# One decoder block on one core: state-space pieces placed at four sums of each mixer pair, norm and operand arithmetic moved from GpSimd to VectorE

## The chip, the cores and the metric

The kernel runs on one core of a Trainium2 chip. The metric is device microseconds from the start to the end of one execution, as a median over runs. The profile is one execution; its times are microseconds (us) from the start of its span. PE is TensorE, DVE is VectorE, ACT is ScalarE, POOL is GpSimd, and SP is the engine that here only issues DMAs.

## The reference

The block works on 1024 tokens of 1024 features, all in float32:

```
x = LN1(ALPHA*x + 0.5*swiglu(x, ffn1_w_in, ffn1_w_out))
mix = token_mixer(x)                    # proj = x @ mix_w_in, 4096 columns in six parts:
    z      = causal_conv3(cc * ch)      #   short convolution branch
    y_conv = (cb * z) @ conv_w_out
    s      = gelu(s5_scan(su))          #   diagonal state-space branch, 32 groups of 64 states
    y_ssm  = ga * sigmoid(gb)           #   ga, gb = split(s @ w_glu)
    out    = (sigmoid(g_conv)*y_conv + sigmoid(g_ssm)*y_ssm) @ mix_w_out
x = LN2(ALPHA*x + mix)
x = LN3(ALPHA*x + 0.5*swiglu(x, ffn2_w_in, ffn2_w_out))
x = LN4(ALPHA*x + (p @ ple_w_in) * sigmoid(x @ ple_w_gate))
```

## The kernel before

**Arithmetic.** Every float32 product is made of three passes of PE: each operand is split into a rounded high part (ACT, L175) and the remainder as a low part (DVE, L176, `Wl` for weights, `x..l` for activations), and PE adds high by high, high by low and low by high. A weight block `Ws` is loaded by SP, becomes `Wh` on ACT and then `Wl` on DVE, with three buffers of each, and only then can PE finish the product that uses it.

**Pairs.** The two feed-forward inputs and the mixer's input projection are computed by a Winograd scheme (class `Pair`) of seven products of 12 matmuls each for two column blocks. POOL forms the sums of weights (`s`, L79, L84, L88, L96), DVE adds the products up in four sums (L87, L92, L99, L101). The activations need seven operands `x11`, `xt1`, `xt2`, `xt3`, `x21`, `x22`, `xt4`; four of them are differences of blocks. For the first feed-forward they come from DMA and are formed in `first_operands.later` (L422 to L438) at some 17 to 50 us: one half of them (j = 0) on DVE, one half (j = 1) on POOL. For the mixer and for the second feed-forward they are formed in `winograd_sink` while the norm ahead of them ends (two sinks, some 695 to 750 us and 1280 to 1335 us): here j = 0 is POOL's, j = 1 DVE's.

**Mixer.** 16 pairs: two for the state-space input, four gates, six for the convolution, four gates. Into these pairs the state-space branch is fed in pieces: `ssm_quarter` is a generator with 12 steps for each of four quarters, and after each pair from the second on the loop takes three steps (four from the eleventh on). After the last pair the region "ssm" is closed and "res2" opened in its place, into which the eight blocks `gc` are loaded (`acc<-gc`, L1061, 512 KB each). Then come the products with `conv_w_out`, whose weights are `in_w_co`, and the state-space result `s` is loaded and split to `sT`.

**Last loop.** For each of eight rows of 128 tokens (in two cuts of 512 columns, in three for the last) PE forms the gate `pg` (24 matmuls, L1243) and the embedding `pe` (6 matmuls, L1248, two PSUM buffers `pt`), ACT the sigmoid `sg` (L1251), DVE the product (L1252) and the sum into `acc2` (L1253), and then the row's norm. Ahead of that, `affine(...)`'s `apply` multiplies the row by the third norm's gain and adds its bias (L315, L316), the left half on DVE, the right half on POOL.

**Order.** The code is written in order, and a scheduler of the tile framework then places the instructions of all engines by its own estimate of when each is ready. `tc.issue_after(ins)` keeps what is written inside it behind `ins` on that instruction's engine; without it the scheduler may hoist work ahead of other rows'. DMAs are all issued by SP, in one order, and SP waits at each for what that DMA needs.

Of the kernel before, what the change touches and what calls it, by code (L numbers as in the profile page):

```python
# [12 lines left out]
ALU = mybir.AluOpType  # L13
# [8 lines left out]
EARLY = 5  # L22
FIRST = [f for i in range(NPAIR) for f in (i, NPAIR + i)]
MAGIC = 12582912.0
TICKS = 3
HALVES = (slice(0, 512), slice(512, 1024))


# [77 lines left out]
class Block:  # L106
# [194 lines left out]
    def affine(self, g, b, tag):  # L301

        if tag == "A8":
            both = self.t("A8", [P, 2, D], name="gb")
            gb = [both[:, v, 512 * h:512 * h + 512] for v in range(2) for h in range(2)]
        else:
            gb = [self.t(tag, [P, 512], name="gb") for _ in range(4)]
        for i, part in enumerate(gb):
            self.nc.sync.dma_start(part, (g, b)[i // 2][i % 2 * 512:i % 2 * 512 + 512].partition_broadcast(P))

        def apply(t):
            for h in range(2):
                sl = slice(h * 512, (h + 1) * 512)
                eng = (self.nc.vector, self.nc.gpsimd)[h]
                eng.tensor_tensor(t[:, sl], t[:, sl], gb[h], ALU.mult)  # L315
                eng.tensor_tensor(t[:, sl], t[:, sl], gb[2 + h], ALU.add)  # L316
        return apply


# [20 lines left out]
    def winograd_sink(self, xs, gb):  # L340

        kept = []
        gps = self.nc.gpsimd

        def put(name, y, i, j, eng=None):
            cols, ks = slice((i % 2) * 256, (i % 2 + 1) * 256), slice(2 * j, 2 * j + 2)
            hi, lo = xs[name]
            self.split(y, hi[:, ks, cols], lo[:, ks, cols], eng)

        def sink(i, pair):  # L350
            if i < 2:
                kept.append([self.t("H", [P, 4, 256], name="y") for _ in range(2)])
                for kh in range(2):
                    for j in range(2):
                        y = kept[i][kh][:, 2 * j:2 * j + 2]
                        self.features(pair, gb, 4 * kh + 2 * j, y)
                        put(("11", "21")[kh], y, i, j, None if (kh, j) == (0, 1) else gps)
                return
            for j in range(2):
                b11, b21 = (kept[i - 2][kh][:, 2 * j:2 * j + 2] for kh in range(2))  # L360
                b12, b22 = self.t("T", [P, 2, 256], name="b12"), self.t("T", [P, 2, 256], name="b22")
                t1 = self.t("T", [P, 2, 256], name="t1")
                self.features(pair, gb, 2 * j, b12)
                eng = (gps, self.nc.vector)[j]
                eng.tensor_tensor(t1, b12, b11, ALU.subtract)
                put("t1", t1, i, j)
                self.features(pair, gb, 4 + 2 * j, b22)
                put("22", b22, i, j)
                eng.tensor_tensor(b12, b22, b12, ALU.subtract)
                put("t3", b12, i, j)  # L370
                eng.tensor_tensor(t1, b22, t1, ALU.subtract)
                put("t2", t1, i, j)
                eng.tensor_tensor(t1, b21, t1, ALU.subtract)
                put("t4", t1, i, j)
        return sink
# [4 lines left out]
    def first_operands(self, xT, w_in):  # L380

        nc = self.nc
        xs = self.new_xs()
        self.open_region("init")
        p, w = {}, {}
        early = FIRST[:EARLY]

        def weight(f, kh):
            w[f, kh] = self.stage(w_in[f][kh])

        def piece(n, j):
            kh, th = int(n[0]) - 1, int(n[1]) - 1
            p[n, j] = self.r("xp", [P, 2, 512], 8)
            return xT[:, kh, th, 2 * j:2 * j + 2, :]

        def put(n, j, y, ks=slice(0, 2)):
            hi, lo = xs[n]
            k0 = slice(2 * j + ks.start, 2 * j + ks.stop)
            self.split(y[:, ks], hi[:, k0], lo[:, k0])

        weight(early[0], 0)
        for j in range(2):
            src = piece("11", j)
            for k in range(2):
                ks = slice(k, k + 1)
                nc.sync.dma_start(p["11", j][:, ks], src[:, ks])
                put("11", j, p["11", j], ks)
            weight(early[1 + j], 0)
        for f in early[3:]:
            weight(f, 0)  # L410
        for j in range(2):
            src = piece("21", j)
            nc.sync.dma_start(p["21", j], src)
            put("21", j, p["21", j])
        for n in ("12", "22"):
            for f in (early[:2] if n == "12" else early[2:]):
                weight(f, 1)
            for j in range(2):
                src = piece(n, j)
                nc.sync.dma_start(p[n, j], src)  # L420

        def later():  # L422
            tt = [self.t("H", [P, 2, 512], name="t1") for _ in range(2)]
            eng = (nc.vector, nc.gpsimd)
            for j in range(2):
                eng[j].tensor_tensor(tt[j], p["12", j], p["11", j], ALU.subtract)
                put("t1", j, tt[j])
            for j in range(2):
                eng[j].tensor_tensor(tt[j], p["22", j], tt[j], ALU.subtract)
                put("t2", j, tt[j])  # L430
            for j in range(2):
                eng[j].tensor_tensor(p["12", j], p["22", j], p["12", j], ALU.subtract)
                put("t3", j, p["12", j])
            for j in range(2):
                put("22", j, p["22", j])
            for j in range(2):
                eng[j].tensor_tensor(tt[j], p["21", j], tt[j], ALU.subtract)
                put("t4", j, tt[j])  # L438
        return xs, w, later

# [544 lines left out]
    def mixer(self, xs, a, acc):  # L985
        nc = self.nc
        vec, gps = nc.vector, nc.gpsimd
# [30 lines left out]
        order += [("gs", i, i + 1) for i in (24, 26, 28, 30)]  # L1018
        base = {"su": (12, su_d), "gc": (16, gc_d), "gs": (24, gs_d)}
        pieces = iter(())  # L1020
        pairs = self.in_pairs([lambda o=o: make(*o) for o in order])
        for n, ((kind, i, j), p) in enumerate(zip(order, pairs)):
            p.rest()
            parts = [(0, 1, p.a2), (1, 0, p.c1), (1, 1, p.c2)]
            if kind == "conv":
                self.conv(p, zs, i - 4)
            elif kind == "cb":
                for k, h, t in parts:
                    z = zs[k][:, halves[h]]
                    vec.tensor_tensor(z, t, z, ALU.mult)  # L1030
                for k in range(2):
                    nc.sync.dma_start(q_d[i + k], zs[k])
            else:
                first, dst = base[kind]
                for k, h, t in [(0, 0, p.a1)] + parts:
                    if kind != "su" and t is not p.a1:
                        nc.scalar.activation(t, t, AF.Sigmoid)
                    nc.sync.dma_start(dst[i - first + k][:, halves[h]], t)
            if n == 1:
                self.open_region("ssm")  # L1040
                pieces = (None for q in range(4) for _ in self.ssm_quarter(q, su_d[q], s_d[q]))
            for _ in range(TICKS + (n > 9)):
                next(pieces, None)

        def load_pair(src, name):
# [13 lines left out]
        for dt in range(8):  # L1059
# [3 lines left out]
            for h in range(2):  # L1063
                t = m[:, halves[h]]
# [16 lines left out]
        for dt in range(8):  # L1081
# [9 lines left out]
            gb, ga = (product(a["w_glu"][i], sT) for i in (8 + dt, dt))  # L1091
            for h in range(2):
                sg = self.t("T", [P, 512], name="sg")
# [18 lines left out]
        gb = self.t("A8", [P, 2, D], name="gb")  # L1112
# [36 lines left out]
    def run(self, a, out):  # L1149
        nc = self.nc  # L1150
# [41 lines left out]
        acc2, last = self.mixer(state["x"], a, acc)  # L1192
# [31 lines left out]
        for v in ("ln4_g", "ln4_b"):  # L1224
            for h in range(2):
                tl = self.t("Ws", [P, 512], name="gb4")
                nc.sync.dma_start(tl, a[v][h * 512:(h + 1) * 512].partition_broadcast(P))
                gb4.append(tl)
        for s in range(NT):
            cols = slice((s % 4) * P, (s % 4 + 1) * P)  # L1230
            if s % 2 == 0:
                pp = self.split_w(self.stage(a["pT"][:, s // 2]))
            apply(acc2[s])
            pcol = lambda k: slice((2 * (s % 2) + k) * P, (2 * (s % 2) + k + 1) * P)
            cuts = HALVES if s < NT - 1 else (slice(0, 512), slice(512, 768), slice(768, D))
            for sl in cuts:
# [8 lines left out]
                pe = self.pt()[:, :n]  # L1245
# [3 lines left out]
                                         stop=(k == 1 and i == 2))  # L1249
                sg = self.t("T", [P, 512], name="sg")[:, :n]  # L1250
                nc.scalar.activation(sg, pg, AF.Sigmoid)  # L1251
                nc.vector.tensor_tensor(sg, pe, sg, ALU.mult)  # L1252
                nc.vector.scalar_tensor_tensor(acc2[s][:, sl], sg, 1.0 / ALPHA, acc2[s][:, sl], ALU.mult, ALU.add)  # L1253
            mean, y, _ = self.moments(acc2[s], cuts)
            for dh, sl in enumerate(HALVES):
# [66 lines left out]
```

## Time and profile before

| | |
|---|---|
| median of three runs | 2084.79 us (2083.38 to 2086.32) |
| the profiled execution, its own time | 2086.58 us |
| its span | 2084.8 us |
| busy: PE, DVE, POOL, ACT | 2001.7, 1668.0, 846.4, 813.7 us |
| granted TensorE clock, mean | 0.991 of full speed |

The span is the time from the first to the last recorded instruction. PE is busy for 96% of it, so all that other engines can hold up is the rest and the stretches in which PE runs at half its clock. 1.00 in the column PEclk is 2.4 GHz.

### The profile page before, as it was taken

The numbers are of one execution on the slowest core, as the hardware profiler recorded it, in microseconds if no ns is written. First come the engines' busy times: TensorE is split into PE (matmuls) and PEld (weight loads), VectorE is DVE, ScalarE is ACT, GpSimd is POOL, SyncE is SP. The second block draws the span as 40 slices with busy tenths as digits, with TensorE's granted clock in tenths as the row PEclk, the third lists the DMA queues.
The fourth block names the chain that finished last, engine by engine and source line by source line (L and its number), as shares of the span: only waits on it lengthen the run. The fifth ranks groups of instructions, "written<-read, shape, count | busy, mean of one in ns | idle before, by whom it ended". The sixth has DMA issues, their size and how long they took to land.

```text
span 2084.8 us, 26465 instructions
## 1 busy us (share of the span) xinstructions
PE 2001.7 (96%) x9030; PEld 1633.4 (78%) x9030; DVE 1668.0 (80%) x2560; ACT 813.7 (39%) x1422; POOL 846.4 (41%) x562
## 2 busy tenths in 40 slices
PE   7999999999999899999999999999999999999988
PEld 5887778776788777887878888788888876788867
DVE  7789888879998976767644679877667789998897
ACT  5333343445342545343533415533333345342520
POOL 3644444454313454333201372654444444313360
PEclk9999999999999999999999999999999999999999
DMA  4433343556540264333382410243323246431111
GB/s 170 127 117 96 122 141 126 179 186 223 164 141 25 106 187 148 100 122 114 133 299 80 151 53 17 83 149 117 101 87 126 91 166 217 162 128 69 54 45 69
DMA packets 153238, 260.24 MB, mean 125 GB/s; under 512 B 16144, under 2 KB 61200, under 8 KB 153104
## 3 DMA queue, kind: packets, MB, share of 16 engines
q1 hardware_dynamic: 153104, 258.56, 37.6%
q8 instruction: 71, 1.16, 0.2%
q14 instruction: 63, 0.52, 0.1%
HBM read 189.85 MB, written 68.65 MB: 124 GB/s over the span
## 4 chain that ended last, share of the span: by engine, by line
PE 67%; DVE 21%; issue 5%; DMA 2%; ACT 2%; POOL 2%; SPq 0%; DVEq 0%; POOLq 0%; ACTq 0%
PE pm L198 42%; PE pm L615 11%; PE pm L209 5%; PE pm L229 5%; DVE Wl L176 4%; PE pm L1243 2%; DVE wt L176 2%; DVE w L176 1%; DVE acc L622 1%; DVE ln L254 1%; PE pt L1248 1%; DVE ln L248 1%; DVE ln L255 1%; DVE acc L316 1%; DVE acc L234 1%
## 5 line engine op out<-in xcount | busy, mean ns | idle before, releaser
L175 ACT CAST Wh<-Ws 128x512 fp32r<-128x512 f32 x268 | 166.6, 622 | 346.5 <-PE pm L198 277.5
L176 DVE TENSOR_TENSOR Wl<-Ws,Wh 128x512 fp32r<-128x512 f32 x268 | 212.8, 799 | 109.1 <-ACT Wh L175 108.7
L175 ACT CAST Wh<-s 128x512 fp32r<-128x512 f32 x240 | 149.2, 622 | 379.2 <-PE pm L198 139.3
L176 DVE TENSOR_TENSOR Wl<-s,Wh 128x512 fp32r<-128x512 f32 x240 | 213.5, 890 | 25.8 <-ACT Wh L175 25.7
L615 PE MATMUL pm<-wt,Wh 128*128 128x512 f32 x640 | 188.0, 392 | 2.5 <-DVE acc L622 2.5
L84 POOL TENSOR_TENSOR s<-s,Ws 128x512 f32<-128x512 f32 x60 | 90.2, 1503 | 203.6 <-DVE Wl L176 193.3
L102 POOL TENSOR_TENSOR u<-u,p 128x512 f32<-128x512 f32 x60 | 96.1, 1602 | 144.3 <-DVE u L92 93.2
L615 PE MATMUL pm<-w,Wh 128*128 128x512 f32 x480 | 141.4, 392 | 6.1 <-ACT Wh L175 5.5
L622 DVE SCALAR_TENSOR_TENSOR acc<-pm,acc 128x512 f32<-128x512 f32 x200 | 132.7, 682 | 15.5 <-PE pm L615 14.8
L615 PEld LDWEIGHTS pm<-wt,Wh 128*128 128x128 f32 x640 | 119.7, 188 | 30.2 <-DVE acc L622 3.3
L79 POOL TENSOR_TENSOR s<-Ws 128x512 f32<-128x512 f32 x60 | 82.5, 1374 | 133.8 <-DVE Wl L176 102.0
L96 POOL TENSOR_TENSOR s<-Ws,s 128x512 f32<-128x512 f32 x60 | 92.3, 1538 | 108.8 <-DVE Wl L176 107.4
L615 PE MATMUL pm<-wt,Wl 128*128 128x512 f32 x320 | 113.8, 394 | 3.9 <-DVE Wl L176 3.6
L615 PEld LDWEIGHTS pm<-w,Wh 128*128 128x128 f32 x480 | 90.0, 189 | 26.8 <-ACT Wh L175 7.1
L198 PE MATMUL pm<-x11h,Wh 128*128 128x512 f32 (+1 forms) x264 | 99.1, 384 | 5.0 <-ACT x11h L175 5.0
L198 PE MATMUL pm<-x11h,Wl 128*128 128x512 f32 (+1 forms) x264 | 99.3, 379 | 3.1 <-DVE Wl L176 3.1
L198 PE MATMUL pm<-x11l,Wh 128*128 128x512 f32 (+1 forms) x264 | 99.6, 380 | 1.9 <-DVE x11l L176 1.3
L198 PE MATMUL pm<-xt1h,Wl 128*128 128x512 f32 x240 | 95.3, 397 | 5.3 <-DVE Wl L176 5.3
L198 PE MATMUL pm<-x21h,Wl 128*128 128x512 f32 x240 | 95.1, 396 | 5.5 <-DVE Wl L176 5.5
L198 PE MATMUL pm<-xt2h,Wl 128*128 128x512 f32 x240 | 94.8, 395 | 4.2 <-DVE Wl L176 4.1
L198 PE MATMUL pm<-xt4h,Wl 128*128 128x512 f32 x240 | 94.1, 392 | 4.6 <-DVE Wl L176 4.6
L198 PE MATMUL pm<-xt1l,Wh 128*128 128x512 f32 x240 | 94.4, 393 | 2.1 <-DVE xt1l L176 2.1
(355 smaller groups left out, 5615.7 us busy)
## 6 DMA issues: line engine op xcount, KB each, us to landing
Ws<-in_ffn_w_in SPq DMA_DIRECT2D x196, 256.0 KB, 2.7
Ws<-in_ffn_w_out SPq DMA_DIRECT2D x88, 256.0 KB, 3.1
Ws<-in_w_mix SPq DMA_DIRECT2D x74, 256.0 KB, 2.7
s<-h_s SPq DMA_DIRECT2D x60, 256.0 KB, 3.0
h<-a SPq DMA_DIRECT2D x58, 256.0 KB, 2.3
ha<-h SPq DMA_DIRECT2D x20, 512.0 KB, 4.1
hb<-h SPq DMA_DIRECT2D x20, 512.0 KB, 4.6
h_s<-u SPq DMA_DIRECT2D x20, 256.0 KB, 2.6
```

What stands on the lines that cost most here:

```text
L79: gps.tensor_tensor(s, a21, a22, ALU.add)
L84: gps.tensor_tensor(s, s, a11, ALU.subtract)
L96: gps.tensor_tensor(s, a12, s, ALU.subtract)
L102: gps.tensor_tensor(u3, u3, p5, ALU.add)
L175: self.nc.scalar.copy(hi, src)
L176: (lo_eng or self.nc.vector).tensor_tensor(lo, src, hi.bitcast(F32), ALU.subtract)
L198: self.nc.tensor.matmul(ps[:, tok], w[a][:, sl], x[b](k)[:, tok], start=(start and k == 0 and i == 0), stop=(k == nk - 1 and i == 2), skip ...
L209: self.nc.tensor.matmul(ps[h], w[a][:, sl], x(h)[b](k), start=(k == 0 and i == 0), stop=(k == 3 and i == 2))
L229: nc.tensor.matmul(ps, a[:, s * P:(s + 1) * P], b[:, cols], start=(j == 0 and i == 0), stop=(j == n - 1 and i == 2))
L615: nc.tensor.matmul(ps[i], hh[p][:, cols], w[n][:, j, q], start=(start and j == 0 and k == 0), stop=(j == 1 and k == 2), skip_group_check=n ...
L622: vec.scalar_tensor_tensor(t, ps[i], scale, t, ALU.mult, ALU.add)
L1243: nc.tensor.matmul(pg, xx[p](k % 4)[:, cols], wg[dh][k][q][:, col], start=(k == 0 and i == 0), stop=(k == NK - 1 and i == 2))
```

## The change

Four edits. The third norm's factor and bias (`apply`) are all on DVE, and each row's is put behind the last `sg` product of the row before. The j = 1 differences of the first feed-forward, and the j = 0 differences of the two sinks, go to DVE too. In the mixer one piece of the state-space branch is taken behind each of a pair's four sums, inside `p.rest`, instead of three after the pair; one more after the pair remains from the eleventh on.

```diff
         def apply(t):
+            vec = self.nc.vector
             for h in range(2):
                 sl = slice(h * 512, (h + 1) * 512)
-                eng = (self.nc.vector, self.nc.gpsimd)[h]
-                eng.tensor_tensor(t[:, sl], t[:, sl], gb[h], ALU.mult)
-                eng.tensor_tensor(t[:, sl], t[:, sl], gb[2 + h], ALU.add)
+                vec.tensor_tensor(t[:, sl], t[:, sl], gb[h], ALU.mult)
+                vec.tensor_tensor(t[:, sl], t[:, sl], gb[2 + h], ALU.add)
...
                 self.features(pair, gb, 2 * j, b12)
-                eng = (gps, self.nc.vector)[j]
+                eng = self.nc.vector
                 eng.tensor_tensor(t1, b12, b11, ALU.subtract)
...
             tt = [self.t("H", [P, 2, 512], name="t1") for _ in range(2)]
-            eng = (nc.vector, nc.gpsimd)
+            vec = nc.vector
             for j in range(2):
-                eng[j].tensor_tensor(tt[j], p["12", j], p["11", j], ALU.subtract)
+                vec.tensor_tensor(tt[j], p["12", j], p["11", j], ALU.subtract)
                 put("t1", j, tt[j])
...
+        def tick(ins):
+            with self.tc.issue_after(ins.ins):
+                next(pieces, None)
+
         pairs = self.in_pairs([lambda o=o: make(*o) for o in order])
         for n, ((kind, i, j), p) in enumerate(zip(order, pairs)):
-            p.rest()
+            p.rest(tick)
...
-            for _ in range(TICKS + (n > 9)):
+            if n > 9:
                 next(pieces, None)
...
+        last = None
         for s in range(NT):
...
-            apply(acc2[s])
+
+            with self.tc.issue_after(last.ins) if last else ExitStack():
+                apply(acc2[s])
...
-                nc.vector.tensor_tensor(sg, pe, sg, ALU.mult)
+                last = nc.vector.tensor_tensor(sg, pe, sg, ALU.mult)
```

The other three differences in `later` change in the same way. In the rows below, line numbers of the changed kernel are one lower than before up to the mixer and four to seven higher behind it.

DVE at the start of the last loop, before (`acc<-acc,gb` is `apply`, a multiplication at L315 and an addition at L316; `sg<-pt,sg` the gate's product):

```order
L176 TENSOR_TENSOR Wl<-Ws,Wh 128x512 x3
L315 TENSOR_TENSOR acc<-acc,gb 128x512 x8
L316 TENSOR_TENSOR acc<-acc,gb 128x512 x3
L1252 TENSOR_TENSOR sg<-pt,sg 128x512
L316 TENSOR_TENSOR acc<-acc,gb 128x512 x2
L1252 TENSOR_TENSOR sg<-pt,sg 128x512
L316 TENSOR_TENSOR acc<-acc,gb 128x512 x3
L1253 SCALAR_TENSOR_TENSOR acc<-sg,acc 128x512
```

The same place in the changed kernel:

```order
L175 TENSOR_TENSOR Wl<-Ws,Wh 128x512 x3
L314 TENSOR_TENSOR acc<-acc,gb 128x512 x2
L315 TENSOR_TENSOR acc<-acc,gb 128x512
L1259 TENSOR_TENSOR sg<-pt,sg 128x512
L315 TENSOR_TENSOR acc<-acc,gb 128x512
L1260 SCALAR_TENSOR_TENSOR acc<-sg,acc 128x512
L1259 TENSOR_TENSOR sg<-pt,sg 128x512
L314 TENSOR_TENSOR acc<-acc,gb 128x512 x2
```

Eleven operations stood ahead of the first `sg` product; now three do, and the second row's follow behind the second product. POOL had 16 such operations here and has none now.

DVE at the operand differences of the start, before (`t_349` and `t_350` are the two halves' differences, L429, L432 and L437 those of j = 0 alone, since j = 1 was POOL's; `Wl<-s` is the split of the first weight sum, which the product with `xt1` needs):

```order
L429 TENSOR_TENSOR t_349<-xp,t_349 128x1024
L432 TENSOR_TENSOR xp<-xp 128x1024
L176 TENSOR_TENSOR Wl<-Ws,Wh 128x512
L176 TENSOR_TENSOR xt2l<-t_349,xt2h 128x1024
L176 TENSOR_TENSOR Wl<-Ws,Wh 128x512
L437 TENSOR_TENSOR t_349<-xp,t_349 128x1024
L176 TENSOR_TENSOR xt3l<-xp,xt3h 128x1024
L176 TENSOR_TENSOR xt2l<-t_350,xt2h 128x1024
L176 TENSOR_TENSOR Wl<-Ws,Wh 128x512
L176 TENSOR_TENSOR x22l<-xp,x22h 128x1024 x2
L176 TENSOR_TENSOR xt3l<-xp,xt3h 128x1024
L176 TENSOR_TENSOR Wl<-s,Wh 128x512
```

In the changed kernel, the last twelve rows up to the same split:

```order
L175 TENSOR_TENSOR Wl<-Ws,Wh 128x512
L428 TENSOR_TENSOR t_350<-xp,t_350 128x1024
L431 TENSOR_TENSOR xp<-xp 128x1024
L175 TENSOR_TENSOR Wl<-Ws,Wh 128x512
L175 TENSOR_TENSOR xt2l<-t_349,xt2h 128x1024
L175 TENSOR_TENSOR xt3l<-xp,xt3h 128x1024
L175 TENSOR_TENSOR Wl<-Ws,Wh 128x512
L175 TENSOR_TENSOR xt2l<-t_350,xt2h 128x1024
L436 TENSOR_TENSOR t_349<-xp,t_349 128x1024
L175 TENSOR_TENSOR x22l<-xp,x22h 128x1024 x2
L175 TENSOR_TENSOR xt3l<-xp,xt3h 128x1024
L175 TENSOR_TENSOR Wl<-s,Wh 128x512
```

Counted from the first difference (`t_349<-xp`) to `Wl<-s`, DVE had 12 operations of 128x1024 and 6 of 128x512; now it has 15 and 6, the fourth moved one (`t_350` of L436) stands right behind.

SP at the end of the mixer's pairs, before (`acc<-gc` are the last two of eight loads; `s_6376<-st` stores the state-space result's last quarter, `Ws<-s_6376` loads it):

```order
L1061 DMA acc<-gc_6383 128x1024
L1061 DMA acc<-gc_6384 128x1024
L981 DMA s_6376<-st 128x512
L1089 DMA mt<-gs_6392 128x1024
L981 DMA s_6376<-st 128x512
L180 DMA Ws<-s_6376 128x512 x2
L180 DMA Ws<-in_w_co 128x512 x4
```

In the changed kernel around the same two loads:

```order
L1065 DMA acc<-gc_6383 128x1024
L1065 DMA acc<-gc_6384 128x1024
L179 DMA Ws<-in_w_mix 128x512
L1042 DMA gs_6388<-u_8909 128x512
L980 DMA s_6376<-st 128x512 x2
L1042 DMA gs_6387<-a_8943 128x512
L1042 DMA gs_6387<-a_8962 128x512
L179 DMA Ws<-in_w_mix 128x512
L1042 DMA gs_6388<-u_8838 128x512
L179 DMA Ws<-in_w_mix 128x512
```

The eight loads and the last quarter's stores stood behind all pairs' weights; now all eight, one behind the other, stand ahead of the last three weight blocks (`in_w_mix`) of the last pair, and the stores ahead of its last two.

## Rows read from the trace of the kernel before

**Rows 1.** The page, busy time, share of the span and instructions of each engine.

```profile
PE 2001.7 (96%) x9030; PEld 1633.4 (78%) x9030; DVE 1668.0 (80%) x2560; ACT 813.7 (39%) x1422; POOL 846.4 (41%) x562
```

**Rows 2.** PE's waits over the whole span: total, times, longest.

```profile
PE pm L198 <- DVE Wl L176: 24.6, 24, 3.2
```

**Rows 3.** Last loop, timeline of DVE, POOL, PE: start, duration, idle before and releaser.

```profile
1986.06 13.54 DVE L315 TENSOR_TENSOR acc<-acc,gb 128x512 f32<-128x512 f32 x8 [1.19 <-DMA gb<-in_ln_g]
...
1988.84 13.55 POOL L315 TENSOR_TENSOR acc<-acc,gb 128x512 f32<-128x512 f32 x8
...
1988.31 0.50 PE L1243 MATMUL pm<-wgh,xh 128*128 128x512 f32 x1 [0.83 <-ACT sg L1251]
...
2005.27 1.22 PE L1248 MATMUL pt<-wp,Wh 128*128 128x512 f32 x2 [7.14 <-DVE sg L1252]
...
2016.14 1.07 PE L1248 MATMUL pt<-wp,Wh 128*128 128x512 f32 x2 [2.03 <-DVE sg L1252]
```

**Rows 4.** Last loop by stretches: busy of PE, PEld, DVE, ACT, POOL; PEclk; DMA share; GB/s.

```profile
2005.00:2010.00 5.00, 4.73 (x12) 3.79 (x13) 5.00 (x6) 0.00 (x0) 5.00 (x4) 0.55 0.00 0
...
2015.00:2020.00 5.00, 3.86 (x10) 3.04 (x11) 4.97 (x9) 2.48 (x5) 0.89 (x1) 0.66 0.00 0
2020.00:2025.00 5.00, 5.00 (x24) 4.10 (x23) 5.00 (x14) 0.60 (x1) 0.00 (x0) 1.00 0.00 0
```

**Rows 5.** The whole last loop from DVE's first `apply`, same columns.

```profile
1986.06:2085.00 98.94, 79.72 (x361) 65.70 (x359) 87.97 (x172) 11.62 (x20) 29.82 (x18) 0.91 0.13 49
```

**Rows 6.** PE's waits from 12 to 62 us.

```profile
PE pm L198 <- DVE Wl L176: 6.8, 4, 3.2
```

**Rows 7.** Start, timeline of DVE and PE.

```profile
16.95 3.49 DVE L426 TENSOR_TENSOR t<-xp 128x1024 f32<-128x1024 f32 x1
...
24.65 1.22 DVE L429 TENSOR_TENSOR t<-xp,t 128x1024 f32<-128x1024 f32 x1
...
46.25 0.50 PE L198 MATMUL pm<-xt1h,Wl 128*128 128x512 f32 x1 [3.20 <-DVE Wl L176]
```

**Rows 8.** First sink, DVE's and POOL's timelines.

```profile
708.25 1.66 DVE L265 TENSOR_SCALAR acc<-acc,ln 128x1024 f32<-128x1024 f32 x1
...
716.68 1.28 DVE L176 TENSOR_TENSOR Wl<-Ws,Wh 128x512 fp32r<-128x512 f32 x2
...
725.52 1.57 DVE L176 TENSOR_TENSOR Wl<-Ws,Wh 128x512 fp32r<-128x512 f32 x1 [2.74 <-ACT Wh L175]
...
742.13 1.77 DVE L176 TENSOR_TENSOR x22l<-b,x22h 128x512 fp32r<-128x512 f32 x1
...
716.84 7.09 POOL L371 TENSOR_TENSOR t<-b,t 128x512 f32<-128x512 f32 x1 [3.84 <-DVE xt1l L176]
```

**Rows 9.** First sink, busy by engine from 690 to 755 us.

```profile
690.00:755.00 65.00, 55.01 (x283) 43.47 (x281) 61.17 (x107) 43.78 (x85) 37.75 (x21) 0.97 0.44 148
```

**Rows 10.** PE's waits for `Wl`, 690 to 770 us, then 1280 to 1345 us.

```profile
PE pm L198 <- DVE Wl L176: 3.5, 4, 1.4
...
PE pm L198 <- DVE Wl L176: 3.8, 3, 2.3
```

**Rows 11.** Mixer, one pair: timelines of DVE and PE; then POOL at the last pair.

```profile
959.56 1.77 DVE L952 TENSOR_TENSOR T<-RR,RS 128x508 f32<-128x508 f32 x1
...
963.18 0.50 PE L198 MATMUL pm<-xt4h,Wl 128*128 128x512 f32 x1 [1.65 <-DVE Wl L176]
...
1018.49 1.29 POOL L79 TENSOR_TENSOR s<-Ws 128x512 f32<-128x512 f32 x1 [7.67 <-DVE Wl L176]
```

**Rows 12.** Behind the mixer's pairs, timelines of SP, ACT and PE.

```profile
1062.72 1.16 SPq L981 DMA_DIRECT2D s<-st  x1
...
1074.88 0.62 ACT L175 CAST sT<-Ws 128x512 fp32r<-128x512 f32 x1 [14.18 <-DMA Ws<-s]
...
1078.14 3.44 PE L209 MATMUL pm<-qT,Wh 128*128 128x512 f32 x8 [2.91 <-ACT Wh L175]
```

**Rows 13.** The stretch in which the eight loads run, columns as in rows 4.

```profile
1060.00:1065.00 5.00, 5.00 (x24) 4.13 (x23) 1.91 (x4) 0.70 (x2) 0.00 (x0) 1.00 0.95 296
```

More of the change, by code (lines that the diff above doesn't have):

```diff
@@ L24 @@
 MAGIC = 12582912.0
-TICKS = 3
 HALVES = (slice(0, 512), slice(512, 1024))
@@ L423, in later @@
             tt = [self.t("H", [P, 2, 512], name="t1") for _ in range(2)]
-            eng = (nc.vector, nc.gpsimd)
+            vec = nc.vector
             for j in range(2):
-                eng[j].tensor_tensor(tt[j], p["12", j], p["11", j], ALU.subtract)
+                vec.tensor_tensor(tt[j], p["12", j], p["11", j], ALU.subtract)
                 put("t1", j, tt[j])
             for j in range(2):
-                eng[j].tensor_tensor(tt[j], p["22", j], tt[j], ALU.subtract)
+                vec.tensor_tensor(tt[j], p["22", j], tt[j], ALU.subtract)
                 put("t2", j, tt[j])
             for j in range(2):
-                eng[j].tensor_tensor(p["12", j], p["22", j], p["12", j], ALU.subtract)
+                vec.tensor_tensor(p["12", j], p["22", j], p["12", j], ALU.subtract)
                 put("t3", j, p["12", j])
@@ L436, in later @@
             for j in range(2):
-                eng[j].tensor_tensor(tt[j], p["21", j], tt[j], ALU.subtract)
+                vec.tensor_tensor(tt[j], p["21", j], tt[j], ALU.subtract)
                 put("t4", j, tt[j])
```

## The prediction, made before the changed kernel ran

> **What bounds the kernel.** The first view is the busy time: PE has work for 96% of the span and DVE for 80% [rows 1], so PE sets the pace and whatever the change gains must come out of the 83 us in which PE is idle, and out of stretches at half clock. The second is the table of PE's waits. Its largest line, 24.6 us in 24 waits, is weight splits on DVE that come late [rows 2]; it is a sum over stages, so I looked where it falls. It falls where DVE and POOL work on the same data at the same time: the start [rows 6], the two sinks [rows 10] and the last loop [rows 3]. The timelines show why. A DVE operation of 128x512 takes 0.60 us in a run of its own (two in 1.28) and 1.77 us beside a POOL operation [rows 8]; one of 128x1024 takes 1.22 alone, 1.13 in a run, and 3.49 us beside one [rows 7]. So where both engines form halves of one thing, its own half costs DVE what both would.
>
> **The last loop.** Before it, DVE has eight multiplications that take 13.54 us while POOL does its eight in 13.55 [rows 3]. The additions follow in the same way, and PE waits 7.14 and 2.03 us for `sg`. After the first wait PE is busy for 4.73 us at a granted clock of 0.55 of 2.4 GHz, mostly its lower level, and gets 12 matmuls done where a full stretch has 24: 4.73 x 0.45 = 2.1 us lost. After the second it is 3.86 us at 0.66, 1.3 lost [rows 4]. Together 7.14 + 2.03 + 2.1 + 1.3 = 12.6, taken as 12.5 us. In the changed order three operations (1.8 us from 1986.06) stand ahead of the first `sg`, so it ends near 1988.9, when ACT has its sigmoid; PE, which starts at 1988.31 [rows 3], has 22 matmuls or 5 us ahead of the one that needs it. Can DVE keep up? It is busy for 88.0 us from 1986.06 on [rows 5]. 16 operations of 13.54/8 = 1.69 us go (27.1), 32 of 0.60 come (19.2): 80.1 us. PE now ends at 1986.06 + 79.72 busy + 0.83 + 7.14 + 2.03 waiting = 2075.8 [rows 3, 5], which leaves 9.0 us of the span for the last norm and store, an estimated 6 of them DVE's. If PE loses nothing it ends at 2063.3; 74 us of DVE work in the 77 us from 1986.06 until then fits, barely. Counted along both orders, each `sg` is done 4 us or more before PE wants its buffer. **12.5 us; bounds 9 (DVE's rest of 3 us used up) and 13.3 (the wait of 0.83 gone too).**
>
> **The start.** PE waits 6.8 us in four places, last for `Wl<-s` at 46.25 [rows 6, 7]. From DVE's first difference at 16.95 to that split there were 12 operations of 128x1024 and 6 of 128x512, alone 12 x 1.13 + 6 x 0.60 = 17.2 us; they took 29. Now there are 15 and 6, 20.6 us, and POOL's four differences are gone; two of its weight sums stay in that stretch and cost DVE some 1.2 each, as between 0.60 and 1.77 [rows 8], so the split is done near 16.95 + 20.6 + 2.4 = 40. PE without its waits would be there at 46.25 - 6.8 = 39.5 at the latest. So it resumes at 40 instead of 46.25: **6 us**. It is the lower bound 2 if the added operations that now stand ahead of earlier `Wl` hold those up as long as the stretching did, and 9 if PE never waits.
>
> **The two sinks.** In the first, DVE is busy for 61.2 of 65 us [rows 9]. Seven DVE operations, from the one at 708.25 (1.66) to the one at 742.13 (1.77) [rows 8], are stretched by the POOL operations that move, by 6.9 us in all. Taking over eight operations of 0.60 costs 4.8, so DVE gains 2.1. Another 2.74 us go with POOL's 7.09: ACT waits for that operation's result, with the split for 725.52 queued behind it on ACT [rows 8]. So DVE gains 4.8, PE can gain no more than it waits, which for `Wl` is 3.5 here and 3.8 in the second sink [rows 10], with shorter waits for `x..l` and `Wh` beside them. I take **3.3 us each**. Below: 0, if the j = 0 differences, which now stand ahead of early splits, take back what the stretching took. Above: 5.5.
>
> The Trainium skill (SBUF — State Buffer, "Who interferes with whom") says that a DVE instruction with two SBUF inputs and a GpSimd instruction that reads SBUF hold the shared ports exclusively, and that the loser blocks fully until the other has finished. By that each moved operation could cost DVE a whole POOL operation, 1.29 us, and moving eight would give 8 x (1.29 - 0.60) = 5.5 us a sink in place of 2.1. The rows show smaller losses, and one of the eight cost DVE nothing while POOL's operation took 7.09.
>
> **The mixer's pairs.** The pieces are as much DVE work as before. They stand one by one behind the four sums rather than three or four together; at 963.18 PE waits 1.65 us because four operations of a piece pair (one of them 1.77) stand ahead of a split [rows 11]. It is the largest of a few. Half of them may go, others may come: **1 us; bounds -3 and 4**.
>
> **Behind the pairs.** The last quarter's store is issued at 1062.72, behind eight loads `acc<-gc` of 512 KB each, which keep the DMA engines 95% busy at 296 GB/s [rows 13]; its load back waits for it, ACT waits 14.18 us for that and PE 2.91 [rows 12]. With four pieces a pair the branch ends two pairs earlier, the stores and the loads run beside pair 15, and this wait is gone. With the half clock that follows a wait of this size (1.3 after 2.03 us in the last loop) that is some 4 us. The price: the eight loads, 4 MB, now stand in SP's queue ahead of pair 15's last three weight blocks. POOL starts that pair's first sum at 1018.49 [rows 11]; the loads stand in the place of weights that are fetched most of a pair ahead (84 matmuls, some 18 us at 24 in 5 us), so I estimate a lead of 15 us, and at 296 GB/s they need 14. I charge 1 us: **3 us; bounds -2 and 5**.
>
> **The sum.** 12.5 + 6 + 3.3 + 3.3 + 1 + 3 = 29 us from the profiled execution's 2086.6 gives 2057.5. That execution is 1.8 us above the median of the runs, so 2055.7; I say 2056. Fewer changes of ACT's function table come with the new order of pieces; ACT is busy for 39% [rows 1] and I count nothing.
>
> **Rivals.** *DVE becomes the bound where it takes over work.* For it: 61.2 of 65 us busy [rows 9] and new operations ahead of early splits. Against it: the stretching that goes is larger than the added work at each place. Then start and sinks together give 2 in place of 12.6 and the rest stays: 2056 + 10.6 = 2066 us.
>
> *The eight loads hold up the last pair.* Its sums wait for weights behind 4 MB. For it, DMA engines 95% busy by these loads alone [rows 13]; against it, the lead of about 15 us. A wait of 5 us with the clock behind it would give 2056 + 6 = 2062 us. The Trainium skill (DMA: Bandwidth & Descriptors, "Queues, rings and completion order") says that on each DMA engine descriptors are consumed in ring order; by this rule the weights wait for all of the 4 MB, which is this rival. Nothing in the trace of before has a small load behind such a burst with PE in need of it.
>
> *POOL starves, and the kernel becomes slower.* POOL's operation at 716.84 took 7.09 us instead of 1.29 while DVE ran back to back [rows 8], 5.8 us late. The change makes DVE denser in every pair of the mixer, and POOL's weight sums feed four of a pair's seven products. One such starvation in a pair, less the lead of one product (12 matmuls, 2.5 us [rows 4]), costs PE 3.3 us; if it comes in nine or more of the 14 pairs it outweighs the 29 us, and in all 14 the time is 2056 + 46 = 2102 us. Against it: POOL has slack in the pairs (idle for 7.67 us ahead of 1018.49 [rows 11]), and a piece is short.
>
> *The last loop does not do what it says.* If the scheduler's order lets DVE fall behind PE later, the wait reappears in the middle; DVE's 3 us of rest say that it can be a few us, and then the sum is 2056 + 6 = 2062. If start and sinks fail as well, the gain is about that of no change that a measurement could tell, 2080 or above.
>
> **How the numbers follow.** The forecast, 2047 to 2063, has 0.60. DVE as the bound of start and sinks 0.16, the loads 0.10, the last loop falling behind 0.07; these three give 2060 to 2070. Starved POOL 0.04, several at once without a gain 0.03. The range holds the first and the better part of the next three: 2046 to 2068. About 0.2% (4.2 us) is what a measurement of this kernel can tell from no change: faster by more has 0.60 + 0.16 + 0.10 + 0.07 = 0.93, within it 0.03, slower 0.04.
>
> **What would show it.** In the profile after: PE's waits for `sg` of the last loop gone and PEclk at 1.00 there; the first product with `xt1` at about 40; PE's `Wl` waits of the two sinks near zero; no wait behind the mixer's pairs and `s<-st` issued before 1020. The prediction is wrong where DVE waits nowhere in the last loop and PE waits for `pt`, where PE waits for `Wh<-s` with a long POOL operation ahead of it, or where pair 15 waits for its weights.

## The result, and the profile after

The changed kernel takes 2057.14 us (median of four runs, 2055.71 to 2057.76) beside 2085.03 for the kernel before: a ratio of 0.9866, 95% interval 0.9849 to 0.9883. Timed again with later experiments it took 2056.68 (0.9865, 0.9849 to 0.9882). The forecast was 2056, with 2046 to 2068 as its range.

The page's first part for the changed kernel answers to [rows 1]. POOL lost 52 us of busy time and DVE, which took over its work, lost 13 all the same:

```profile
PE 1992.9 (97%) x9030; PEld 1631.0 (79%) x9030; DVE 1654.7 (81%) x2596; ACT 807.2 (39%) x1418; POOL 794.1 (39%) x526
```

PE's waits over the span (total, times, longest); the first line was 24.6 [rows 2], and the line for DVE's `sg` in the last loop, 9.2 us before, is gone. Of the two lines for `Wh` the second was 5.5 before; the first was 1.3 and is what now stands out:

```profile
PE pm L197 <- DVE Wl L175: 15.6, 18, 3.3
...
PE pm L197 <- ACT Wh L174: 5.9, 4, 3.9
PE pm L614 <- ACT Wh L174: 5.9, 3, 2.8
```

Where the time went is read from PE's timeline at the same instruction in both kernels, at places between which the order of PE is the same or nearly so. The kernel before (the places in the start and at the last loop are in [rows 7] and [rows 3]):

```profile
706.04 0.90 PE L281 MATMUL pt<-ident,acc 128*128 128x128 f32 x3 [2.07 <-DVE acc L265]
...
764.41 0.39 PE L198 MATMUL pm<-x22h,Wh 128*128 128x512 f32 x1
...
1074.62 0.61 PE L209 MATMUL pm<-qT,Wl 128*128 128x512 f32 x2
...
1284.94 0.33 PE L281 MATMUL pt<-ident,acc 128*128 128x128 f32 x1 [0.30 <-ACT y L283]
```

The changed kernel:

```profile
40.29 0.50 PE L197 MATMUL pm<-xt1h,Wl 128*128 128x512 f32 x1 [3.26 <-DVE Wl L175]
...
702.02 0.90 PE L280 MATMUL pt<-ident,acc 128*128 128x128 f32 x3 [2.08 <-DVE acc L264]
...
757.64 0.39 PE L197 MATMUL pm<-x22h,Wh 128*128 128x512 f32 x1
...
1066.19 0.62 PE L208 MATMUL pm<-qT,Wl 128*128 128x512 f32 x2
...
1271.96 0.33 PE L280 MATMUL pt<-ident,acc 128*128 128x128 f32 x1 [0.30 <-ACT y L282]
...
1971.77 0.50 PE L1250 MATMUL pm<-wgh,xh 128*128 128x512 f32 x1 [0.79 <-ACT sg L1258]
```

So the changed kernel leads by 46.25 - 40.29 = 6.0 us in the start, by 4.0 when the first sink begins, by 6.8 behind it, by 8.4 behind the mixer's pairs (just ahead of the wait of 2.91 in the kernel before), by 13.0 when the second sink begins, by 16.5 at the last loop and by 29.7 at the span's end (2084.8 and 2055.1). By stage: start 6.0, of which 1.9 are lost again by the first sink; first sink 2.8; mixer with what follows 6.2, of which 1.7 in the pairs; second sink with the feed-forward behind it 3.6; last loop 13.2.

In the last loop DVE now works without POOL beside it (timeline of DVE; the first row's 3.05 us is the only stretched one, with POOL still splitting `xl`):

```profile
1969.84 3.05 DVE L314 TENSOR_TENSOR acc<-acc,gb 128x512 f32<-128x512 f32 x2 [1.68 <-DMA gb<-in_ln_g]
1972.82 0.68 DVE L315 TENSOR_TENSOR acc<-acc,gb 128x512 f32<-128x512 f32 x1
1973.42 0.68 DVE L1259 TENSOR_TENSOR sg<-pt,sg 128x512 f32<-128x512 f32 x1
```

It is busy for 80.1 us from there to the end where it was 88.0 [rows 5], and PEclk is 1.00 at 1985 to 1990, where behind PE's first wait it was 0.55 [rows 4] (busy of PE, PEld, DVE, ACT, POOL; PEclk; DMA share; GB/s). What keeps the mean of the whole loop at 0.96 is its end: from 2040 on PEclk is 0.79, with PE busy for 5.9 of 16 us.

```profile
1985.00:1990.00 5.00, 5.00 (x24) 4.14 (x23) 5.00 (x11) 0.91 (x2) 0.00 (x0) 1.00 0.00 0
...
1969.50:2056.00 86.50, 75.65 (x361) 63.31 (x359) 80.14 (x188) 11.96 (x20) 2.84 (x2) 0.96 0.15 56
```

Behind the mixer's pairs the wait of 2.91 [rows 12] is gone, and PE waits for nothing from 990 to 1100. SP's timeline shows the eight loads, the last pair's next weights and the stores, which were issued at 1062.72 before:

```profile
995.41 4.33 SPq L1065 DMA_DIRECT2D acc<-gc  x8
999.84 0.39 SPq L179 DMA_DIRECT2D Ws<-in_w_mix  x1
...
1002.57 1.55 SPq L980 DMA_DIRECT2D s<-st  x2
```

The six weight loads that SP issues from 985 to 1015 take this long to land; the longest is the one issued right behind the eight loads, at 999.84:

```profile
DMA to landing us min/median/max: 2.5/3.6/9.8
```

In the sinks something new shows. POOL's timeline has its weight sums at 11.24, 7.95 and 5.26 us instead of 1.29. The split of the last of them on ACT, and with it PE, waits for it (timelines of POOL, ACT and PE):

```profile
718.66 11.24 POOL L78 TENSOR_TENSOR s<-Ws 128x512 f32<-128x512 f32 x1 [12.51 <-DVE Wl L175]
...
1285.62 7.95 POOL L78 TENSOR_TENSOR s<-Ws 128x512 f32<-128x512 f32 x1 [9.16 <-DMA Ws<-in_ffn_w_in]
...
1299.51 5.26 POOL L83 TENSOR_TENSOR s<-s,Ws 128x512 f32<-128x512 f32 x1 [4.24 <-DVE Wl L175]
...
1304.80 0.62 ACT L174 CAST Wh<-s 128x512 fp32r<-128x512 f32 x1 [4.10 <-POOL s L83]
...
1305.47 0.80 PE L197 MATMUL pm<-xt2h,Wh 128*128 128x512 f32 x1 [3.94 <-ACT Wh L174]
```

### The profile page after: what moved, and what is told of

Its sections match the earlier page's. It is cut to its first block, busy times and chain, and to the rows that moved or that the text cites. A ratio compares the mean times of both kernels' runs of the same rounds, so it can differ in the third digit from the quotient of the medians.

```text
span 2055.1 us, 26444 instructions
## 1 busy us (share of the span) xinstructions
PE 1992.9 (97%) x9030; PEld 1631.0 (79%) x9030; DVE 1654.7 (81%) x2596; ACT 807.2 (39%) x1418; POOL 794.1 (39%) x526
## 4 chain that ended last, share of the span: by engine, by line
PE 70%; DVE 19%; issue 5%; DMA 3%; POOL 2%; ACT 1%; SPq 0%; DVEq 0%; POOLq 0%; ACTq 0%
PE pm L197 42%; PE pm L614 11%; PE pm L208 6%; PE pm L228 5%; DVE Wl L175 3%; PE pm L1250 3%; DVE wt L175 2%; DVE acc L621 2%; DVE w L175 1%; POOL s L78 1%; PE pt L1255 1%; DMA Ws<-in_ffn_w_in 1%; DMA Ws<-in_ffn_w_out 1%; DVE ln L253 1%; DVE ln L247 1%
## 5 line engine op out<-in xcount | busy, mean ns | idle before, releaser
L175 DVE TENSOR_TENSOR Wl<-Ws,Wh 128x512 fp32r<-128x512 f32 x268 | 205.3, 772 | 104.2 <-ACT Wh L174 101.7
L78 POOL TENSOR_TENSOR s<-Ws 128x512 f32<-128x512 f32 x60 | 98.8, 1646 | 176.1 <-DVE Wl L175 103.5
L197 PE MATMUL pm<-xt2h,Wh 128*128 128x512 f32 x240 | 94.2, 392 | 5.7 <-ACT Wh L174 5.7
L197 PE MATMUL pm<-x22h,Wl 128*128 128x512 f32 x240 | 95.1, 396 | 4.6 <-DVE Wl L175 4.6
```

What stands on the lines that cost most here:

```text
L78: gps.tensor_tensor(s, a21, a22, ALU.add)
L175: (lo_eng or self.nc.vector).tensor_tensor(lo, src, hi.bitcast(F32), ALU.subtract)
L197: self.nc.tensor.matmul(ps[:, tok], w[a][:, sl], x[b](k)[:, tok], start=(start and k == 0 and i == 0), stop=(k == nk - 1 and i == 2), skip ...
```

## Experiments

The theory: DVE operations are stretched beside POOL's, and the change gains by taking POOL away (start, sinks, last loop) and by ending the state-space branch earlier (mixer). The rivals: it is the order of the work that counts, in the last loop and in the pairs; or the parts do not add up.

All ratios are to the kernel before, timed beside the kernel named; its median was 2086.0, 2084.8 and 2085.7 in the three sets of runs. Single profiles of one kernel differ: a second one of the changed kernel (run changed_again) has a span of 2051.5 beside 2055.1. So spans are not compared below 4 us. The gains by stage repeat much better. Here they are for six profiles, in us over the kernel before, read from PE's timeline at the instructions shown above:

| profile | start | from there to the first sink | first sink | mixer | second sink and feed-forward | last loop |
|---|---|---|---|---|---|---|
| changed kernel | 6.0 | -1.9 | 2.8 | 6.2 | 3.6 | 13.2 |
| changed_again | 7.1 | -0.5 | 3.6 | 6.2 | 3.7 | 13.2 |
| undo_start | 2.1 | -0.4 | 3.6 | 6.2 | 3.4 | 13.2 |
| undo_sinks | 6.2 | -1.2 | 0.4 | 6.2 | 0.4 | 12.9 |
| undo_last_loop | 6.5 | -2.7 | 3.6 | 6.2 | 2.9 | -0.3 |
| undo_mixer | 6.9 | -3.0 | 3.6 | 2.0 | 2.6 | 13.2 |

The column of the start is the product with `xt1`. Each undo below takes away the gain of its own stage, or most of it, and leaves the others nearly as they were; only the first two columns vary much from profile to profile.

**undo_start.** The j = 1 differences of the start back on POOL.

```diff
-            vec = nc.vector
+            eng = (nc.vector, nc.gpsimd)
...
-                vec.tensor_tensor(tt[j], p["12", j], p["11", j], ALU.subtract)
+                eng[j].tensor_tensor(tt[j], p["12", j], p["11", j], ALU.subtract)
...
```

> The changed kernel with the j = 1 differences of the start back on POOL. If the start was worth what the two traces show there (the first product with xt1 at 40.3 instead of 46.3), and the parts add up, the time is 2057 + 6 = 2063 us and that product is back at about 46. Rival: what the start gives is taken back before the first sink anyway (the lead over the kernel before falls from 5.6 to 4.1 us between 350 and 560 us), then 2057 + 4 = 2061 or less.

2060.22 us (ratio 0.9879, 0.9864 to 0.9893), 3 us more. PE's timeline has the product at

```profile
44.18 0.79 PE L197 MATMUL pm<-xt1h,Wl 128*128 128x512 f32 x1 [3.21 <-DVE Wl L175]
```

3.9 us later than in the changed kernel. PE waits for that split in all three kernels, and about as long (3.20, 3.26 and 3.21 us); what the edit sets is when DVE is done with it. The end of the kernel moves by less: the rival's 4 at most. By itself the ratio is not clear of the changed kernel's interval.

**undo_sinks.** The j = 0 differences of both sinks back on POOL.

```diff
-                eng = self.nc.vector
+                eng = (gps, self.nc.vector)[j]
                 eng.tensor_tensor(t1, b12, b11, ALU.subtract)
```

> The changed kernel with the j = 0 differences of both sinks back on POOL. If contention of the two engines was the loss, each sink costs 3 us again (2.7 and 3.7 by the two traces): 2057 + 6.4 = 2063.5 us. Rival: in the changed kernel POOL's own weight sums starve in the sinks (one takes 11.2 us, others 8.0 and 5.3) because DVE now runs without a gap; then giving work back to POOL loses less, and the time is 2057 to 2060.

2063.22 us (0.9894, 0.9877 to 0.9910), 6 us more, as the theory has it; the interval overlaps that of the changed kernel at its edge, but in the table both sinks lose their gain. PE waits for `xt1l` for 2.5 us in the first sink and for 1.8 in the second (0.4 and 1.8 in the kernel before).

**undo_last_loop.** The last loop as before, both parts of the edit taken back.

```diff
-                vec.tensor_tensor(t[:, sl], t[:, sl], gb[h], ALU.mult)
+                eng.tensor_tensor(t[:, sl], t[:, sl], gb[h], ALU.mult)
...
-            with self.tc.issue_after(last.ins) if last else ExitStack():
-                apply(acc2[s])
+            apply(acc2[s])
```

Here `eng` is DVE for the left half and POOL for the right, as before.

> The changed kernel with the last loop as before: right half on POOL, no place fixed for the rows. By the two traces that loop gave 13.3 us, so 2057 + 13 = 2070 us. Rival: the loop's loss was partly set by when its inputs came, which other edits moved; then under 10 us.

2068.65 us (0.9917, 0.9903 to 0.9932), 11.5 us more; its profile's span is 2068.6, 13.5 more. PE's two waits are back, nearly as long as before (7.14 and 2.03 in [rows 3]):

```profile
1988.78 1.22 PE L1254 MATMUL pt<-wp,Wh 128*128 128x512 f32 x2 [7.13 <-DVE sg L1258]
...
1999.63 0.76 PE L1254 MATMUL pt<-wp,Wh 128*128 128x512 f32 x2 [1.85 <-DVE sg L1258]
```

**loop_pool_half** and **loop_no_place.** Each takes back one of the two parts alone: the first gives the right half to POOL and keeps the rows' places, the second keeps everything on DVE and drops `issue_after`.

```diff
 loop_pool_half
-                vec.tensor_tensor(t[:, sl], t[:, sl], gb[h], ALU.mult)
+                eng.tensor_tensor(t[:, sl], t[:, sl], gb[h], ALU.mult)
...
 loop_no_place
-            with self.tc.issue_after(last.ins) if last else ExitStack():
-                apply(acc2[s])
+            apply(acc2[s])
```

> The changed kernel, with the place of each row's factor behind the last product of the row before, but the right half of it back on POOL, whose own order nothing binds: it does eight multiplications and then eight additions. If the order on DVE is what counts, the first product of the gate is still early (two DVE operations ahead of it) and most of the gain stays: 2057 + 3, at most + 6. If the contention of the two engines is what counts, 16 operations on DVE take 1.7 us instead of 0.6 again and use up DVE's rest of 3 us: 2057 + 8 to + 10.

> The changed kernel, everything of the third norm's factor on DVE, but no place fixed for it, so that 16 of its 32 operations (9.6 us) stand ahead of the first product of the gate and 11 more behind the second. If order counts, PE waits for the gate's product some 3 us twice, with half clock behind it: 2057 + 7 (5 to 9). If contention counts, DVE has the same work free of POOL and the time is 2057 to 2059.

loop_pool_half: 2060.03 us (0.9881, 0.9866 to 0.9896), 3 us more. Of the last loop's 13.2 us 8.0 stay by PE's timeline; the order alone does bring `sg` forward, but DVE's operations are stretched, it waits for POOL's first addition, and falls behind until PE waits once (DVE's and PE's timelines):

```profile
1985.06 1.76 DVE L1260 SCALAR_TENSOR_TENSOR acc<-sg,acc 128x512 f32<-128x512 f32 x1 [1.18 <-POOL acc L315]
...
1995.49 0.84 PE L1255 MATMUL pt<-wp,Wh 128*128 128x512 f32 x2 [2.90 <-DVE sg L1259]
```

loop_no_place: 2057.39 us (0.9870, 0.9854 to 0.9887), no different from the changed kernel. The 7 us expected from the order are not there. DVE does 15 multiplications and an addition first and the first product of the gate at 1981.37, 8 us later than in the changed kernel; but PE comes to the product that needs it only at 1984.70, at 1976.93 in the changed kernel, and does gate products until then, 56 of them where the changed kernel has 22 and the kernel before 42:

```profile
1970.64 10.20 DVE L314 TENSOR_TENSOR acc<-acc,gb 128x512 f32<-128x512 f32 x15 [2.20 <-DMA gb<-in_ln_g]
1980.77 0.67 DVE L315 TENSOR_TENSOR acc<-acc,gb 128x512 f32<-128x512 f32 x1
1981.37 0.67 DVE L1258 TENSOR_TENSOR sg<-pt,sg 128x512 f32<-128x512 f32 x1
...
1984.70 0.61 PE L1254 MATMUL pt<-wp,Wh 128*128 128x512 f32 x2
```

So the scheduler placed PE's instructions later as well. A long block on DVE ahead of `sg` is harmless here as long as its operations take 0.60 us each, not 1.69. In the kernel before the first `sg` stood behind 11 such operations, from 1986.06 on; at 0.60 us each it would by estimate have been done near 1993.3, ahead of PE, which came for it at 1998.1 (2005.27 - 7.14). Its lateness is their stretching. That the scheduler reckons with durations of DVE alone is inferred from these orders; its estimates are not on record. The two parts overlap: all work on DVE alone leaves 12.3 of the 13.2 us, the places alone 8.0.

**undo_mixer** and **four_after_pair.** Both take the pieces out of the pair again; the first with three after each pair as before, the second with four, so that the branch ends as early as in the changed kernel.

```diff
-            p.rest(tick)
+            p.rest()
...
-            if n > 9:
+            for _ in range(3 + (n > 9)):      # four_after_pair: 4 + (n > 9)
                 next(pieces, None)
```

> The changed kernel with three pieces after each pair again (four from the eleventh on) and none behind the sums. By the two traces the mixer and what follows gave 6.2 us: 2057 + 6 = 2063 us, PE waiting some 3 us behind the pairs. Rival: the wait behind the pairs comes back alone, and the pairs themselves are no slower: 2057 + 4 = 2061.

> The changed kernel with four pieces after each pair (five from the eleventh on) and none behind the sums: the branch ends as early as in the changed kernel, only the place differs. If the gain of the mixer is that the branch ends early, so that the loads and stores behind it are not in the way, the time stays: 2057, within 2. If the place behind the sums matters, four pieces together stand ahead of splits, PE waits in the pairs grow from 4.0 us to 7 or more, and the time is 2060 to 2064.

undo_mixer: 2060.66 us (0.9879, 0.9864 to 0.9894), 3.5 us more: the rival's 2061, though by itself not clear of the changed kernel's interval. The wait behind the pairs is back (timelines of ACT and PE, as in [rows 12]), and PE's waits for `Wl` in the pairs are 4.0 us, the same as in the changed kernel:

```profile
1066.88 0.62 ACT L174 CAST sT<-Ws 128x512 fp32r<-128x512 f32 x1 [13.91 <-DMA Ws<-s]
...
1069.96 2.14 PE L208 MATMUL pm<-qT,Wh 128*128 128x512 f32 x8 [2.47 <-ACT Wh L174]
```

four_after_pair: 2054.05 us (0.9853, 0.9838 to 0.9867), not slower than the changed kernel and perhaps faster. Its last stores go out at 991.28, earlier still. PE waits for nothing behind the pairs, and its waits from 755 to 1050 are 2.4 us beside the changed kernel's 4.0 (4 waits there, all for `Wl`):

```profile
PE pm L197 <- DVE Wl L175: 2.0, 3, 1.0
PE pt L967 <- DVE RR L954: 0.4, 1, 0.4
```

The mixer's gain by stage is 7.3 us here, 6.2 with the pieces behind the sums and 2.0 with three after the pair. So the gain is how many pieces a pair takes, not where they stand.

**lead_sums_dve.** The first two weight sums of the first pair, in the mixer and in the second feed-forward, on DVE.

```diff
-        gps.tensor_tensor(s, a21, a22, ALU.add)
+        self.lead[0].tensor_tensor(s, a21, a22, ALU.add)
...
-        gps.tensor_tensor(s, s, a11, ALU.subtract)
+        self.lead[1].tensor_tensor(s, s, a11, ALU.subtract)
...
```

`self.lead` is DVE for these two pairs and POOL for all others.

> The changed kernel with the first two weight sums of the mixer's first pair and of the second feed-forward's first pair on DVE instead of POOL. In the changed kernel these take 11.2, 8.0 and 5.3 us on POOL while DVE runs without a gap, and PE waits 3.94 us for one of them. If starved POOL sums are what is left in the sinks, they go for 0.6 us each on DVE: 2057 - 5 = 2052 us. Rival: DVE is the bound there, and two more operations on it per sink bring as much as they save: 2057 to 2058.

2054.79 us (0.9856, 0.9841 to 0.9871), half of what was expected and not clear of no change. The wait only changed its place: POOL's next operation (L88, the third sum) starves instead, and PE waits 3.05 us for its split where it waited 3.94 for the one before (timelines of POOL and PE):

```profile
718.57 10.66 POOL L88 TENSOR_TENSOR Ws<-Ws 128x512 f32<-128x512 f32 x1 [14.30 <-DVE s L79]
...
1283.66 18.44 POOL L88 TENSOR_TENSOR Ws<-Ws 128x512 f32<-128x512 f32 x1 [10.07 <-DVE s L79]
...
1302.81 0.50 PE L198 MATMUL pm<-xt3h,Wh 128*128 128x512 f32 x1 [3.05 <-ACT Wh L175]
```

DVE's timeline beside it ends its run without a gap at 1300.31 + 0.68 = 1300.99, and POOL's operation ends at 1302.10, 1.1 us behind that:

```profile
1300.31 0.68 DVE L176 TENSOR_TENSOR Wl<-s,Wh 128x512 fp32r<-128x512 f32 x1
1302.79 1.10 DVE L176 TENSOR_TENSOR Wl<-Ws,Wh 128x512 fp32r<-128x512 f32 x1 [1.80 <-ACT Wh L175]
```

**four_lead**, **four_lead_start** and **changed_again.** four_lead is four_after_pair with all four sums of those first pairs on DVE; four_lead_start moves the second sum of the very first pair too; the third is the changed kernel again, beside them.

```diff
+            if i == 0 and later is None:
+                p.lead = (self.nc.vector,) * 4
...
```

> Four pieces after each pair, as in four_after_pair, and all four weight sums of the first pair of the mixer and of the second feed-forward on DVE. With two of the four moved, POOL's next operation there took 10.7 and 18.4 us, as long as DVE had no gap, and PE waited 3.05 us for it. If POOL starving beside a gapless DVE is what is left in the sinks, no POOL operation is wanted there any more: that wait goes, and the time is 2054 - 4 = 2050 us. Rival: DVE's own work is the bound in that stretch; with 2.4 us more of it the time is 2053 to 2056.

> As four_lead, with the second weight sum of the very first pair on DVE as well. In the changed kernel it took 3.33 us on POOL and PE waited 1.45 us for its split. If that wait is POOL's, another 1.5 us go: 2048.5. Rival: DVE is the bound in the start (PE waits 3.26 us there for a split on DVE), and nothing changes: 2050.

> The changed kernel itself, timed beside the two others: 2057 us, within 1.

four_lead: 2049.78 us (0.9829, 0.9812 to 0.9845), clear of the changed kernel beside it (0.9865, 0.9849 to 0.9882) and faster than both kernels of this study. It changes two things at once, but the stages tell them apart: it gains 5.9 us in the first sink and 6.4 from the second sink to the last loop, four_after_pair 3.6 and 4.6. In the second sink POOL has nothing to do from 1271.5 to 1299.59, and PE's wait for `Wh` there is 0.5 us in all (POOL's timeline; PE's waits from 1255 to 1330):

```profile
1299.59 4.09 POOL L79 TENSOR_TENSOR s<-Ws 128x512 f32<-128x512 f32 x1 [28.09 <-DVE Wl L176]
```

```profile
PE pm L198 <- DVE Wl L176: 0.9, 2, 0.5
...
PE pm L198 <- ACT Wh L175: 0.5, 2, 0.4
```

four_lead_start: 2048.31 us (0.9821, 0.9807 to 0.9836). That moving this one sum gains over four_lead is not shown. Its profile lacks the wait of 1.5 us in the start, but so does the second profile of the changed kernel, which has the old code there.

Taken back one at a time, the four parts cost 3, 6, 11.5 and 3.5 us, 24 of the 28. The rest is about what stands in the table as gains that stay with the edit taken back: 2.1 us in the start of undo_start and 2.0 in the mixer of undo_mixer.

## Why the prediction was right, step by step

**The last loop** gave 13.2 us where 12.5 were forecast, at the upper bound. DVE's busy time was forecast at 80.1 us and is 80.14; PE never waits for DVE's `sg`, though the first is done 2.8 us ahead of PE (at 1974.1, beside 1976.93) and not the 4 that were counted. One clause carried less than I gave it: that only three operations stand ahead of the first `sg`. loop_no_place has 16 there and loses less than 1 us of the stage's gain, because PE's order allows for them. The term is mostly that of the stretching.

**The start** gave the 6.0 us at the product with `xt1`, and by the step that was forecast: DVE ends the split at 40.24 (39.56 + 0.68), where "near" 40 was said. PE's wait for it did not shrink (3.26 us, 3.20 before), because PE came earlier too; the waits ahead of it fell from 3.6 us to 0.3. Not all of the 6.0 is the edit's: undo_start, with the old code there, is 2.1 us ahead of the kernel before at this product, so two executions of the same code there differ by that much. What the sum took for granted, that a lead in the start lasts to the end, failed in part: 1.9 of the 6.0 are gone at the first sink, and taking the edit back costs 3 us, not 6. PE's waits from 62 to 690 us are nearly the same in both kernels. What differs there is the clock (the kernel before, then the changed one; columns as above):

```profile
350.00:560.00 210.00, 199.69 (x893) 158.99 (x892) 180.38 (x248) 92.44 (x170) 90.23 (x61) 1.00 0.54 181
350.00:560.00 210.00, 200.56 (x877) 160.00 (x876) 182.43 (x252) 92.08 (x167) 88.35 (x59) 0.98 0.54 180
```

In the changed kernel's profile PEclk falls to half near 462 and again near 503. It is 0.99 over this stretch in undo_start as well, so it is not the start's edit alone that brings this. What does bring it is open.

**The sinks** gave 2.8 and 3.6 us for 3.3 each (3.6 and 3.7 in changed_again); taken back, 6 in both. The stretching is gone as forecast, and with it most of the waits for `Wl` (1.1 and 0.4 us left). But POOL's sums now starve where POOL's differences stood before. That this holds back a further gain is shown by four_lead, which gains 5.9 and 6.4 us in the same stretches.

**The pairs**: 1 us was forecast from "one by one behind the four sums". The size came, 1.7 us, but the step is wrong. The waits for `Wl` are 4.0 us with the pieces in either place; behind the sums they moved, from the product with `xt4` [rows 11] to that with `x22`. With four pieces together after the pair they are 2.0, and the pairs gain 2.8 us; with three, as before, 0.2. So it is the number of pieces again, and why PE then loses less in the pairs no run shows.

**Behind the pairs**: 4 us less 1 for the loads were forecast, and 4.5 came. The wait of 2.91 is gone, and with it the half clock behind it, as forecast; four_after_pair and undo_mixer show that the count of pieces does it. PE does not wait for anything behind the loads, so the price of 1 us was not paid. The half clock explains most of why taking the edit back costs 3.5 us and not 6.2: in undo_mixer PE waits 2.47 us at the same place, but the clock does not fall behind it, while in the kernel before it fell to the lower of its two levels, 1.2 GHz (the kernel before, then undo_mixer; columns as above):

```profile
1078.00:1081.00 3.00, 2.85 (x7) 2.23 (x8) 2.03 (x4) 1.33 (x3) 0.00 (x0) 0.50 0.99 341
...
1070.00:1073.00 3.00, 3.00 (x13) 2.46 (x14) 2.97 (x5) 1.24 (x2) 0.00 (x0) 1.00 1.01 356
```

**The rivals.** DVE did not become the bound of the sinks at once, and the eight loads held up nothing of PE's. The rule on ring order that I named from the Trainium skill (DMA: Bandwidth & Descriptors, "Queues, rings and completion order") can be seen: the trace agrees with it in that the weight block issued right behind the loads took 9.8 us to land where the median is 3.6. It cost PE nothing: the weights still landed before PE wanted them. The rival that came closest is starved POOL, and one sign of being wrong that the prediction named did show: PE waiting for `Wh<-s` with a long POOL operation ahead of it, 3.94 us at 1305.47. It did not come in the pairs, where I put it, but in the second sink, and took about 4 us of PE's time once. In the first sink POOL starved too (11.24 us); what PE lost by it there shows no such wait, only what four_lead gains. The sum came out within 1 us partly by luck, because the errors are of both signs: 1.9 lost behind the start, 2.2 more in the mixer, 0.7 more in the last loop.

## What to carry to other kernels

Two halves of one elementwise step on two engines that slow each other down are not twice as fast: price them with durations from a stretch where both run. An order that fits the durations of one engine alone can leave the waiting engine in the wrong place, as PE in the last loop before. When work moves to the engine that is nearly full, look for what is left on the other one in the same stretch, and see whether that has to move too: with two of four sums moved the wait went to the third, with four it was gone. Before crediting where a piece of side work stands, vary how much of it is done per step with the place held fixed.

## What the runs showed of the hardware

POOL and DVE slow each other in two different ways. In some stretches both go on at 1.69 us for each operation, as if they took turns (last loop before, [rows 3]). In others DVE runs at its full pace of 0.60 us and POOL's one operation waits: 7.09 us before [rows 8], 11.24, 7.95 and 5.26 after, 10.66 and 18.44 in lead_sums_dve. Three of these end 1.1 us after DVE's run does: at 729.90, with DVE's run ending at 728.75; at 1304.77, with 1303.65; at 1302.10, with 1300.99. DVE's timeline of the changed kernel at the first two:

```profile
728.07 0.68 DVE L175 TENSOR_TENSOR xt4l<-t,xt4h 128x512 fp32r<-128x512 f32 x1
730.58 1.23 DVE L175 TENSOR_TENSOR Wl<-s,Wh 128x512 fp32r<-128x512 f32 x1 [1.83 <-ACT Wh L174]
...
1302.97 0.68 DVE L372 TENSOR_TENSOR t<-y,t 128x512 f32<-128x512 f32 x1
1305.45 0.69 DVE L175 TENSOR_TENSOR Wl<-s,Wh 128x512 fp32r<-128x512 f32 x1 [1.80 <-ACT Wh L174]
```

The one of 7.95 us ends at 1293.57, in the middle of DVE's work, and there DVE's next operation starts 0.07 us later than its pace of 0.60 and is itself held up (DVE's timeline):

```profile
1291.73 0.68 DVE L175 TENSOR_TENSOR xt2l<-t,xt2h 128x512 fp32r<-128x512 f32 x1
1292.40 1.72 DVE L368 TENSOR_TENSOR b<-b,b 128x512 f32<-128x512 f32 x1
```

So a starved operation seems to need a gap in DVE's work, if a small one, and then takes about its normal time. The Trainium skill (SBUF — State Buffer, "Who interferes with whom") says that the loser blocks until the other has finished; here it is blocked by a run of up to 28 operations, not by one. What decides between alternating and starving is not settled; no run was made on it.
